# The order of every engine's instructions written out as a table

## The chip, the cores and the metric

The kernel runs on one core of a Trainium2 chip. The core has five engines that work side by side and meet at semaphores: TensorE (PE) for matrix products, VectorE (DVE) and ScalarE (ACT) for elementwise work, GpSimd (POOL), and SyncE (SP), which here only issues DMA transfers. Every engine takes its instructions in one fixed order; one that has to wait holds up all that stand behind it on the same engine. The metric is the device time of the whole program in microseconds; of several executions the median counts.

## What is computed

One inference step of a one-layer decoder for a prompt of 1024 tokens and a sample group of 8 x 8 tokens (1088 columns in all), all in float32:

```python
h = rmsnorm(x, norm_mix)
q, k, v, gu, gv, ga, gb = split_in(h @ w_in)
o = sink_attention(...)             # window of 128, 16 heads on 4 key heads, learned sinks
vn = layernorm(gelu(gv), ln_g, ln_b)
s = spatial_gating(gelu(gu), vn, ws, bs)       # 128 x 128 lower triangles, 6 groups
merged = sigmoid(ga) * (o @ w_pa) + sigmoid(gb) * (s @ w_pb)
x = x + merged @ w_out
f = conv_ffn(rmsnorm(x, norm_ffn), ...)        # up, causal conv of width 3, gelu gate, down
y = rmsnorm(x + f, norm_final)
```

Besides y the new keys, values, convolution rows and normalised v rows are returned.

## The kernel before

Activations lie with features on the 128 partitions and tokens along the free dimension. A float32 product is made of three products of rounded halves: `split` writes hi, a copy by ACT (L41), and lo = src - hi, by DVE (also L41), for weights (`wh`, `wl`), activations (`th`, `tl`, `t` for both in one tile) and softmax results (`ph`, `pl`). PE then adds wh*hi, wh*lo and wl*hi.

The large products save multiplications: seven products of half-sized blocks instead of eight (class `Chain`). A chain works on 288 tokens (group 0, tiles `t`) or 256 (group 1, `th`, `tl`); with both groups two chains take turns. Product j writes the PSUM bank given by the j-th letter of "adadaca", so j=2, 4 and 6 go on in the bank of j=0. Before PE may go on there, ACT has copied the sum so far out of it (`keep`, L296 and L298: `k1`, `k5`, `ku`, and `kn` with the sign changed). DVE adds finished parts into `z` (L303, L339), ACT copies others (L343).

The stages in order: v and gv token by token (L535); the input chains for ga, gb, q, k, gu (L317), with the layer norm's jobs (L758 to L765: load `v` from DRAM, ACT L759, DVE L761 and L762, store) and the mixing matmuls (L788, L816) woven in between; attention of group 0, then group 1, with pieces of the merge products (L242) between its steps; the output product; the up projection chains (L317) with convolution and gate (L1564 to L1631); the down projection (L1686); the final norm (L1719 to L1772).

One attention step: scores (PE L1182), copy and mask (ACT L1188, DVE L1190), row maximum (DVE L1196), four exponentials (ACT L1199), reciprocal and scaling of `s` (DVE L1201, L1202), transposes (PE L1209) into `pt`, split into `ph` and `pl`, product with the values (PE L1233) into `po`, of which there is one bank; ACT copies one half of it to `ot` (L1238), two DVE additions make `of` (L1243), and a split makes `oh` and `ol`. Merge products leave their bank (`mm`, two of them) by a DVE multiplication into `stg` (L1030 in the branch, L1054 in the merge), which is then stored.

The order of each engine comes from the tile framework's scheduler: it takes the instructions as written and lets those that are ready pass others. A handful are pinned with `keep_in_program_order` (splits of the mixing's results, some additions of the down projection, a table load, the last outputs). DMA transfers are issued by SP in the order so found. Weights are loaded through a ring of raw tiles and split up to three products ahead (`W.get(3, ...)`).

Of the kernel before, what the change touches and what calls it, by code (L numbers as in the profile page):

```python
# [6 lines left out]
F32 = mybir.dt.float32  # L7
F32R = mybir.dt.float32r
I32 = mybir.dt.int32
AF = mybir.ActivationFunctionType  # L10
# [5 lines left out]
P = 128  # L16
# [18 lines left out]
def layer(tc, a):  # L35
    nc = tc.nc
    V, S, G, PE = nc.vector, nc.scalar, nc.gpsimd, nc.tensor

    def split(hi, lo, src, pin=False):

        for x in (S.copy(hi, src), V.tensor_sub(lo, src, hi.bitcast(F32))):  # L41
            if pin:
                tc.keep_in_program_order(x)

# [4 lines left out]
    with ExitStack() as top:  # L49
# [14 lines left out]
        warm = cst.tile([P, 1], F32, name="c_warm")  # L64
# [318 lines left out]
        with ExitStack() as ph1:  # L383
            c1 = ph1.enter_context(tc.tile_pool(name="c1", bufs=1))
# [57 lines left out]
            order = [*range(FEW, 9), 0, *range(9, 15), 1, *range(15, NFF), 2]  # L442
# [14 lines left out]
            def dn_unit(j, i):  # L457
# [12 lines left out]
                def add(to, x, y):  # L470
                    tc.keep_in_program_order(V.tensor_add(to, x, y))
                    return to
# [388 lines left out]
            s_raw = {}  # L861
# [5 lines left out]

            def split_s(g, pool, c, pin=False):
                x = pool.tile([P, 2, groups[g]["n"]], F32R, name=f"s{g}{c}")
                split(x[:, 0], x[:, 1], s_raw.pop(c), pin)  # L870
                ss[g].append((x[:, 0], x[:, 1]))
# [87 lines left out]
            for at, (pair, gs) in enumerate(seq):  # L959
# [12 lines left out]
                for j in range(7):  # L972
                    w = W.get(3, 1 if j < 4 else 4 if at == len(seq) - 1 else 2)
# [87 lines left out]
            def attention(gr, pieces):  # L1061
# [18 lines left out]
                if has_s:  # L1080
                    st = {}

                    def sc_s(kc):
# [19 lines left out]
                        if kc == 0:  # L1103
                            tc.keep_in_program_order(S.activation(warm, s2[:, 3, 0:1], AF.Exp))
                        for lo, hi, m in ((0, P, smp["m"][:, None, 0:P].to_broadcast([P, 4, P])),
# [165 lines left out]
            for c in range(3):  # L1271
                split_s(1, m1, c, True)
                load_s(1, c + 2)
# [363 lines left out]
        for at, f in enumerate(order):  # L1637
# [11 lines left out]
            for j in range(7):  # L1649
                w = W.get(3, 1)  # L1650
# [10 lines left out]
        with ExitStack() as ph3:  # L1661
# [85 lines left out]
            def y_out(th, e, c0, c1):  # L1747
                lo, hi = spans[e]
                w, at = hi - lo, KD * (HT * th + lo)
                tc.keep_in_program_order(  # L1750
                    nc.sync.dma_start(a["y"][:, at + c0 * w:at + c1 * w].rearrange("p (m t) -> p m t", t=w),
                                      x1[c0 // 4, th, e][:, c0 % 4:c0 % 4 + c1 - c0]))

            def fin_copy(th, e, rb):
                rs = lp.tile([P, 288], F32, name="rb", bufs=2)[:, :spans[e][1] - spans[e][0]]
                copy = S.copy(rs, rb[-1])
                if not (th and e):
                    tc.keep_in_program_order(copy)
                return rb[0], rs

            def fin_mul(th, e, by, cs, eng=V):
                w = spans[e][1] - spans[e][0]
                for c in cs:
                    x2 = x1[c // 4, th, e][:, c % 4:c % 4 + 2]
                    x = eng.tensor_mul(x2, x2, by[:, None, :].to_broadcast([P, 2, w]))
                    if eng is V:
                        tc.keep_in_program_order(x)

# [93 lines left out]
        tops.close()  # L1862
        tops.close()


# [89 lines left out]
```

## Time and profile before

| | us |
|---|---|
| median of 3 executions | 1509.08 |
| the three | 1508.57, 1509.08, 1514.09 |
| the profiled execution, its own time | 1507.61 |
| its span in the profile | 1505.9 |
| PE busy | 1491.5 |
| PE loading weights | 1451.8 |
| DVE busy | 1176.4 |
| ACT busy | 856.3 |
| POOL busy | 265.7 |

A timeline row gives the start, the time it took, engine, source line, operation, tile written and tiles read, shape, how many instructions the row merges, and in brackets the idle time before it with what ended that. A window's row gives the stretch, its length, then for PE, weight loads, DVE, ACT and POOL the busy time and the number of instructions, and last the granted clock, the share of time that DMA engines were busy, and GB/s. Names lose their buffer numbers. Ends of matmuls are modelled, so PE counts as busy a little beyond the time in which it takes in columns.

### The profile page before, as it was taken

To read this page: it belongs to the slowest core of one execution; us is meant where nothing else is said; L and a number is where in the kernel's file an instruction comes from. 1 tells how busy PE (TensorE), PEld (TensorE's weight loads), DVE (VectorE), ACT (ScalarE), POOL (GpSimd) and SP (SyncE) were. 2 spreads that over 40 slices of the span, in tenths; PEclk is the share of its full clock that TensorE was granted. 3 is DMA by queue.
4 is the path that set the end of the run, shared out by engine and by line. 5 is a ranking of instruction groups with operands and counts; after the bars stand their busy time and mean duration, and the time that the engine had idled before them with its cause. 6 is when DMAs were issued, how large, how long until landed. Compare 5 with 4: busy or idle time off the path is not lost.

```text
span 1505.9 us, 30082 instructions
## 1 busy us (share of the span) xinstructions
PE 1491.5 (99%) x11508; PEld 1451.8 (96%) x11508; DVE 1176.4 (78%) x1886; ACT 856.3 (57%) x1790; POOL 265.7 (18%) x375
## 2 busy tenths in 40 slices
PE   9999999999999999999999999999999999999998
PEld 9999999999998989998989999999999999999998
DVE  7798776755576887989667988898899888785586
ACT  7657676654465765864443555555555556363464
POOL 0001000110030222320134321332242222000002
PEclk9999999999999999999999999999999999999999
DMA  7688446864779757438988423232242226993453
GB/s 253 225 275 274 155 163 224 243 207 150 239 243 294 219 180 231 162 123 308 335 295 287 141 109 122 98 142 108 83 151 109 84 83 223 326 303 98 113 172 148
DMA packets 134431, 289.88 MB, mean 192 GB/s; under 512 B 15760, under 2 KB 36560, under 8 KB 134288
## 3 DMA queue, kind: packets, MB, share of 16 engines
q1 hardware_dynamic: 134144, 287.96, 56.8%
q8 instruction: 90, 1.47, 0.4%
q14 instruction: 53, 0.43, 0.1%
q10 hardware_dynamic: 144, 0.01, 0.0%
HBM read 198.97 MB, written 90.92 MB: 192 GB/s over the span
## 4 chain that ended last, share of the span: by engine, by line
PE 85%; DVE 5%; ACT 4%; DMA 3%; issue 2%; POOL 1%; SPq 0%; POOLq 0%; ACTq 0%; DVEq 0%
PE st L317 45%; PE dn L1686 14%; PE mm L242 13%; PE st L535 6%; PE po L1233 2%; PE sc L1182 1%; DVE wl L41 1%; PE pt L1209 1%; DMA v<-gvd 1%; PE mx L816 1%; ACT wh L41 1%; ACT s L1199 1%; DMA kd<-q 0%; DMA v<-gvds 0%; DVE v L761 0%
## 5 line engine op out<-in xcount | busy, mean ns | idle before, releaser
L317 PE MATMUL st<-t,wh 128*128 128x288 f32 x2128 | 428.6, 295 | 3.4 <-ACT k L296 2.3
L317 PEld LDWEIGHTS st<-t,wh 128*128 128x128 f32 x2128 | 335.7, 188 | 4.6 <-ACT k L296 3.0
L317 PE MATMUL st<-t,wl 128*128 128x288 f32 x1064 | 312.2, 293 | 0.0
L317 PE MATMUL st<-th,wh 128*128 128x256 f32 x1064 | 296.0, 278 | 0.6 <-ACT k L296 0.5
L317 PE MATMUL st<-tl,wh 128*128 128x256 f32 x1064 | 294.7, 277 | 0.0
L317 PE MATMUL st<-th,wl 128*128 128x256 f32 x1064 | 294.5, 277 | 0.0
L317 PEld LDWEIGHTS st<-th,wh 128*128 128x128 f32 x1064 | 200.0, 188 | 1.9 <-ACT k L296 1.4
L317 PEld LDWEIGHTS st<-t,wl 128*128 128x128 f32 x1064 | 200.1, 188 | 0.0
L317 PEld LDWEIGHTS st<-th,wl 128*128 128x128 f32 x1064 | 199.8, 188 | 0.0
L317 PEld LDWEIGHTS st<-tl,wh 128*128 128x128 f32 x1064 | 199.8, 188 | 0.0
L1686 PE MATMUL dn<-th,wh 128*128 128x288 f32 (+1 forms) x616 | 177.1, 288 | 0.6 <-ACT zb L343 0.6
L1686 PE MATMUL dn<-tl,wh 128*128 128x288 f32 (+1 forms) x616 | 176.8, 287 | 0.0
L41 ACT CAST wh<-wraw 128x512 fp32r<-128x512 f32 (+2 forms) x188 | 129.4, 701 | 82.0 <-DMA wraw<-wt 30.1
L1686 PE MATMUL dn<-th,wl 128*128 128x288 f32 (+1 forms) x616 | 175.3, 285 | 0.0
L41 DVE TENSOR_TENSOR wl<-wraw,wh 128x512 fp32r<-128x512 f32 (+2 forms) x188 | 148.0, 800 | 28.5 <-ACT wh L41 26.2
L41 ACT CAST wh<-ws 128x512 fp32r<-128x512 f32 x168 | 102.5, 621 | 93.9 <-PE st L317 53.0
L41 DVE TENSOR_TENSOR wl<-ws,wh 128x512 fp32r<-128x512 f32 x168 | 117.5, 710 | 44.5 <-ACT wh L41 43.7
L1686 PEld LDWEIGHTS dn<-th,wh 128*128 128x128 f32 x616 | 115.7, 188 | 1.0 <-ACT zb L343 0.8
L1686 PEld LDWEIGHTS dn<-th,wl 128*128 128x128 f32 x616 | 116.1, 188 | 0.1
L1686 PEld LDWEIGHTS dn<-tl,wh 128*128 128x128 f32 x616 | 115.7, 188 | 0.1
L535 PE MATMUL st<-w2h,hh 128*128 128x256 f32 x288 | 80.6, 280 | 0.4 <-ACT rst L501 0.4
L535 PE MATMUL st<-w2h,hl 128*128 128x256 f32 x288 | 80.1, 279 | 0.1
(281 smaller groups left out, 3169.1 us busy)
## 6 DMA issues: line engine op xcount, KB each, us to landing
wraw<-wt SPq DMA_DIRECT2D x137, 512.0 KB
traw<-td SPq DMA_DIRECT2D x77, 272.0 KB
td<-za SPq DMA_DIRECT2D x22, 544.0 KB
q<-qd SPq DMA_DIRECT2D x16, 512.0 KB
upd<-hl SPq DMA_DIRECT2D x14, 512.0 KB
td<-t SPq DMA_DIRECT2D x11, 544.0 KB
wpart<-wt SPq DMA_DIRECT2D x22, 256.0 KB
qd<-q SPq DMA_DIRECT2D x8, 576.0 KB
```

The source lines that it names most:

```text
L41: for x in (S.copy(hi, src), V.tensor_sub(lo, src, hi.bitcast(F32))):
L242: PE.matmul(ps[:, lo:lo + c1 - c0], u[:, k, :], v[:, c0:c1], start=(k == 0 and i == 0), stop=(k == nk - 1 and i == 2))
L317: PE.matmul(ps, u[:, kk, :], v, start=first and kk + i == 0, stop=kk == 3 and i == 2, skip_group_check=True)
L535: PE.matmul(ps, u[:, lo:lo + P], v[:, k, :], start=k + i == 0, stop=k == KD - 1 and i == 2)
L816: PE.matmul(ps[:, P * i:P * i + P], vn[:, i], late["wst"][:, c, :], start=True, stop=True)
L1182: PE.matmul(ps[:, h, o0:256], q, kst[kv][:, e, k0:cur + P], start=e == 0, stop=e == 1)
L1199: S.activation(s[:, h], s[:, h], AF.Exp, bias=nm[:, h:h + 1], accum_out=dn[:, h:h + 1])
L1209: PE.transpose(pt[:, h * P:h * P + P], s[:, h, 0:P], ident)
L1233: PE.matmul(po, v[:, kv, :], t, start=e == 0, stop=last)
L1686: PE.matmul(place(m, e), u[:, m, :], v[:, lo:hi], start=new and i + k == 0 and (e == 0 or m % 2 == 0), stop=i == NU - 1 and k == 2, skip_g ...
```

## The change

All calls of `keep_in_program_order` go. After the program is written, a new function binds each engine's instructions into one chain: each depends, without a semaphore, on the one before it in the table's order. A digit of the table says how many places ahead of the next unplaced instruction, in the order as written, the next one is taken from.

```diff
-            if pin:
-                tc.keep_in_program_order(x)
...
-                    tc.keep_in_program_order(S.copy(th, x))
+                    S.copy(th, x)
...
+        issue_order(tc)
+
+def issue_order(tc):
+    import re
+    engines = {}
+    for i in tc.nc.cur_bb.bb.instructions:
+        if not isinstance(i, mybir.BassTilePoolBoundary):
+            engines.setdefault(str(i.engine).split(".")[-1], []).append(i)
+    for name, text in ORDER.items():
+        left, last = engines[name], None
+        steps = []
+        for run, far, one in re.findall(r"\((\d+)\)|\[(\d+)\]|([.0-9a-zA-Z])", text):
+            steps += [0] * int(run) if run else [int(far) if far else max(0, DIGITS.find(one))]
+        for j in steps + [0] * (len(left) - len(steps)):
+            now = left.pop(j)
+            if last is not None:
+                tc.add_manual_dep(
+                    now, last.name,
+                    mybir.DependencyInfo(mybir.DependencyClass.NoSync, mybir.DependencyReason.DATA),
+                    reason="issue order")
+            last = now
+
+ORDER = {
...
+    "Activation": (
+        "1.2(4)b..91.7.1.4..22.1...1(5)223..3(4)1..1.1..1.37..1.3..1..133..1(5)777cc.b..e1e.2.a3.33.22.4."
...
+}
```

What is computed and by which instructions does not change. PE's order is the same row for row. Against the order before, 2 instructions stand elsewhere on POOL, 68 on ACT, 132 on DVE and 28 on SP, counted as the fewest that have to be moved to turn one order into the other. Nearly all pass only a few neighbours. In the listings below line numbers of the changed kernel are one or two lower than before, for lines that the change removes.

ACT in the stage of the input chains, before. `k1_4137` copies a chain's bank `st_4124` after its product j=0; `v_4158` and `v_4242` are the layer norm's activations, `z` and `wh` finished outputs and weight casts:

```order
L343 ACTIVATE z10_3806<-st_3815 128x288
L759 ACTIVATE v_4158<-v_4158,mr_3857,sd_3856 128x768
L852 ACTIVATE z10_3806<-z10_3806 128x576
L343 ACTIVATE z11_3808<-st_3830 128x256
L41 CAST wh_4248<-wraw_3706 128x512
L852 ACTIVATE z11_3808<-z11_3808 128x512
L296 COPY k1_4137<-st_4124 128x288
L759 ACTIVATE v_4242<-v_4242,mr_3857,sd_3856 128x768
```

And now:

```order
L341 ACTIVATE z10_3806<-st_3815 128x288
L850 ACTIVATE z01_3807<-z01_3807 128x512
L294 COPY k1_4137<-st_4124 128x288
L757 ACTIVATE v_4158<-v_4158,mr_3857,sd_3856 128x768
L850 ACTIVATE z10_3806<-z10_3806 128x576
L341 ACTIVATE z11_3808<-st_3830 128x256
L294 COPY k1_4152<-st_4139 128x256
L40 CAST wh_4248<-wraw_3706 128x512
L850 ACTIVATE z11_3808<-z11_3808 128x512
```

The copy has passed the activation of v, two of z, a copy and a weight cast; the other chain's copy `k1_4152` has come forward too. Two more waits of this stage (for `kn_4296` and `k1_4413`) are treated alike: the copies now stand ahead of the activations of `v_4314` and `v_4434`.

DVE in attention, before. `stg_7237` empties a merge product's bank `mm_7302`, `dn` and `s_7324` finish a softmax, `of_7369` reads the bank `po_7351`:

```order
L41 TENSOR_TENSOR pl_7359<-pt_7353,ph_7358 128x512
L1030 TENSOR_TENSOR stg_7237<-stg_7237,mm_7302 128x576
L1201 RECIPROCAL dn_7330<-dn_7330 128x4
L1243 TENSOR_TENSOR of_7369<-po_7351,ot_7367 64x256
L1202 TENSOR_TENSOR s_7324<-s_7324,dn_7330 128x4x128
L1243 TENSOR_TENSOR of_7369<-po_7351,ot_7367 64x256
L1190 COPY_PREDICATED s_7397<-c_mprev_482,sc_7388 128x4x128
L41 TENSOR_TENSOR ol2_6587<-of_7369,oh2_6586 128x2x128
L1196 TENSOR_REDUCE nm_7401<-s_7397 128x4
```

And now:

```order
L41 TENSOR_TENSOR pl_7359<-pt_7353,ph_7358 128x512
L1199 RECIPROCAL dn_7330<-dn_7330 128x4
L1200 TENSOR_TENSOR s_7324<-s_7324,dn_7330 128x4x128
L1241 TENSOR_TENSOR of_7369<-po_7351,ot_7367 64x256 x2
L1188 COPY_PREDICATED s_7397<-c_mprev_482,sc_7388 128x4x128
L41 TENSOR_TENSOR ol2_6587<-of_7369,oh2_6586 128x2x128
L1194 TENSOR_REDUCE nm_7401<-s_7397 128x4
L1028 TENSOR_TENSOR stg_7237<-stg_7237,mm_7302 128x576
```

The bank's evacuation went from the front to the end of the step, and `s` ahead of both halves of `of`. Other steps of attention change likewise; the six evacuations `stg` that move back pass 4 to 17 places, and weight splits up to 5.

ACT between the last up projection chain and the down projection, before. `zb_16256` copies the chain's last sum out of `st_16265`, `c_16596` is a convolution's first step:

```order
L41 CAST th_16490<-traw_16405 128x544
L41 CAST wh_16496<-wraw_16419 128x512
L1564 ACTIVATE c_16596<-za_16255,cw_11020 128x1104
L343 ACTIVATE zb_16256<-st_16265 128x256
L41 CAST wh_16496<-wraw_16494 128x512
```

And now:

```order
L40 CAST th_16490<-traw_16405 128x544
L40 CAST wh_16496<-wraw_16419 128x512
L341 ACTIVATE zb_16256<-st_16265 128x256
L1562 ACTIVATE c_16596<-za_16255,cw_11020 128x1104
L40 CAST wh_16496<-wraw_16494 128x512
```

The copy and the convolution have changed places. On SP, at the program's start, the load of the second feature block `x1` has passed the load of the second part of `x0`; later a number of loads pass stores that wait for results, by one to six places.

More of the change, by code (lines that the diff above doesn't have):

```diff
@@ L37, in layer, with split @@
     V, S, G, PE = nc.vector, nc.scalar, nc.gpsimd, nc.tensor
-    def split(hi, lo, src, pin=False):
-        for x in (S.copy(hi, src), V.tensor_sub(lo, src, hi.bitcast(F32))):
-            if pin:
-                tc.keep_in_program_order(x)
+    def split(hi, lo, src):
+        S.copy(hi, src)
+        V.tensor_sub(lo, src, hi.bitcast(F32))
     def scale_split(hi, lo, src, by):
@@ L1103, in sc_s @@
                         if kc == 0:
[L1104 removed]
+                            S.activation(warm, s2[:, 3, 0:1], AF.Exp)
                         for lo, hi, m in ((0, P, smp["m"][:, None, 0:P].to_broadcast([P, 4, P])),
@@ L1749, in y_out @@
                 w, at = hi - lo, KD * (HT * th + lo)
[L1750 to L1752 removed]
+                nc.sync.dma_start(a["y"][:, at + c0 * w:at + c1 * w].rearrange("p (m t) -> p m t", t=w),
+                                  x1[c0 // 4, th, e][:, c0 % 4:c0 % 4 + c1 - c0])
             def fin_copy(th, e, rb):
                 rs = lp.tile([P, 288], F32, name="rb", bufs=2)[:, :spans[e][1] - spans[e][0]]
[L1756 to L1758 removed]
+                S.copy(rs, rb[-1])
                 return rb[0], rs
```

73 lines of the change are left out of this document (66 added, 7 removed).

## The prediction

> **What bounds the kernel now.** I read the page first, then the list of waits of TensorE (PE), then the timeline around each wait. The page's span, its row of busy times, and the last row of PE's timeline:
>
> ```profile
> span 1505.9 us, 30082 instructions
> ...
> PE 1491.5 (99%) x11508; PEld 1451.8 (96%) x11508; DVE 1176.4 (78%) x1886; ACT 856.3 (57%) x1790; POOL 265.7 (18%) x375
> ...
> 1499.66 0.61 PE L1731 MATMUL fs<-c_ident,rt 128*128 128x128 f32 x4
> ```
>
> PE is busy for 1491.5 of 1505.9 us, so all that any order of the other engines can win is in the 14.4 us of idle PE and in what "busy" conceals. The last matmul is over at 1500.3; the 5.6 us behind it are the output's. The waits of PE, whole span (who waited, for whom, us, times, longest):
>
> ```profile
> PE st L317 <- ACT k L296: 2.8, 4, 1.5
> PE st L590 <- DVE c_ones L69: 1.2, 1, 1.2
> PE st L317 <- ACT kn L298: 1.0, 1, 1.0
> PE pt L1209 <- DVE s L1202: 0.6, 2, 0.4
> PE dn L1686 <- ACT zb L343: 0.6, 1, 0.6
> PE fs L1731 <- DVE rt L1723: 0.6, 1, 0.6
> PE pt L1123 <- DVE s L1116: 0.4, 1, 0.4
> PE st L535 <- ACT rst L501: 0.4, 1, 0.4
> PE mm L242 <- DVE x1g L1360: 0.2, 1, 0.2
> PE po L1233 <- DVE of L1243: 0.2, 1, 0.2
> ```
>
> Of these 8.0 us, the memset at the start (c_ones), rst and rt stay as they are: 2.2 us. The other seven rows, 5.8 us in 11 waits, are all for PSUM evacuations or softmax results of ScalarE (ACT) and VectorE (DVE), and the new table puts just these ahead of neighbours. So the question is how much of 5.8 us comes free, and what each wait costs beyond its listed idle time.
>
> Four rows of PE's timeline show the second thing:
>
> ```profile
> 293.74 0.28 PE L317 MATMUL st<-tl,wh 128*128 128x256 f32 x1
> 293.86 0.28 PE L317 MATMUL st<-th,wl 128*128 128x256 f32 x1
> 294.99 0.53 PE L317 MATMUL st<-t,wh 128*128 128x288 f32 x2 [0.86 <-ACT k L296]
> 295.37 0.29 PE L317 MATMUL st<-t,wl 128*128 128x288 f32 x1
> ```
>
> Matmuls of 256 columns start 0.12 us apart, so the next was due at 293.98 and came 1.01 late, not 0.86: a listed wait hides about 0.15. After it two matmuls take 0.38 where two of 288 columns take about 0.26 when PE runs through: another 0.12. I count each listed wait as its idle time plus 0.27.
>
> **Stage 280 to 330 us: minus 4.2.** Here the first pass of seven-product chains runs (one product per j, two chains), while the layer norm's jobs use the same ACT. Two windows, all engines:
>
> ```profile
> 230.00:280.00 50.00, 50.00 (x411) 50.00 (x411) 33.37 (x61) 29.87 (x61) 4.28 (x4) 1.00 0.68 229
> 280.00:330.00 50.00, 46.64 (x374) 45.90 (x374) 35.15 (x49) 28.06 (x55) 7.59 (x7) 1.00 0.73 223
> ```
>
> 411 matmuls in 50 us is 0.122 each; 374 need 45.5, so 4.5 us are lost. From the listed waits: two for k (2.3) and one for kn (1.0), 3.3 + 3 x 0.27 = 4.1. ACT rows from the approach to the three waits:
>
> ```profile
> 290.92 0.63 ACT L852 ACTIVATE z<-z 128x512 f32<-128x512 f32 x1 [0.85 <-DVE z L303]
> ...
> 294.55 0.39 ACT L296 COPY k<-st 128x288 f32<-128x288 f32 x1
> ...
> 303.69 1.03 ACT L759 ACTIVATE v<-v,mr,sd 128x768 f32<-128x768 f32 x1 [4.83 <-DMA v<-gvd]
> ...
> 307.74 0.67 ACT L298 ACTIVATE kn<-st 128x288 f32<-128x288 f32 x2
> ...
> 315.85 1.03 ACT L759 ACTIVATE v<-v,mr,sd 128x768 f32<-128x768 f32 x1 [1.18 <-DMA v<-gvd]
> ```
>
> The k copy of j=0 frees the bank in which j=2 goes on. Between the end of its product and the stall PE ran the other chain's j=0 and both chains' j=1, 36 matmuls x 0.122 = 4.4 us, so the copy could have run from 289.6 on and waited for nothing but its place. In the new order it stands right behind the row of 290.92, about 291.5, and PE asks for it at 293.98: the wait goes whole. kn frees a bank in the same way. It now stands ahead of the activation that waits for a transfer until 303.69; its first half ends at 308.1 (two copies in 0.67 from 307.74), the stall began 1.3 before, its product 4.4 before that, at about 302.4, so it runs some 5 us earlier. The third wait, the longest, is for a k behind the activation of 315.85; k goes ahead of it, more than 2.5 us earlier for a stall of 1.5 + 0.15, and that activation falls nine places back. What is late next is the layer norm's v, read by the mixing matmuls of a later stage. Between 4.1 and 4.5 I take 4.2.
>
> **Attention, 460 to 670 us: minus 3.1.** The edit repeats one pattern. DVE and PE rows of one step:
>
> ```profile
> 542.54 0.76 DVE L1030 TENSOR_TENSOR stg<-stg,mm 128x576 f32<-128x576 f32 x1 [0.45 <-PE mm L242]
> ...
> 543.65 0.42 DVE L1243 TENSOR_TENSOR of<-po,ot 64x256 f32<-64x256 f32 x1 [0.27 <-ACT ot L1238]
> 543.99 0.68 DVE L1202 TENSOR_TENSOR s<-s,dn 128x512 f32<-128x512 f32 x1
> 544.70 0.42 DVE L1243 TENSOR_TENSOR of<-po,ot 64x256 f32<-64x256 f32 x1
> ...
> 544.81 0.30 PE L1209 MATMUL pt<-c_ident,s 128*128 128x128 f32 x1
> 545.26 0.47 PE L1233 MATMUL po<-ph,vst 128*128 128x512 f32 x1
> ```
>
> The transposes at 544.81 wait for s, the matmul at 545.26 for the second of, which frees the one po bank. Now reciprocal and s go first (s over by about 543.4), both of follow (over by about 544.4 instead of 545.1), and stg, whose result is only stored, comes last: this step gains some 0.5. Listed for such steps are s 0.6 and 0.4 and of 0.2, four waits: 1.2 + 4 x 0.27 = 2.3. The wait at 544.81 is under 0.15 and not listed; there are many like it. The page leaves at most 14.4 - 8.0 - 5.6 = 0.8 us of unlisted idle time, and each hides its 0.15 as well, so I bound them by 0 and 2 here and take 1.0, near the middle, as the step above has one of each. One of the two s waits loses only one short DVE instruction ahead of it, so I leave 0.2 of it. 2.3 + 1.0 - 0.2 = 3.1.
>
> **Single places elsewhere: minus 3.1.** The two other k waits, 2.8 - 2.3 = 0.5 + 2 x 0.27 = 1.0; x1g 0.2 + 0.27 = 0.5; unlisted ones before further k copies and in the tail, 0 to 2, taken as 1.0 like those above. The zb wait is different:
>
> ```profile
> 1264.80 1.32 ACT L1564 ACTIVATE c<-za,cw 128x1104 f32<-128x1104 f32 x1
> 1266.01 0.37 ACT L343 ACTIVATE zb<-st 128x256 f32<-128x256 f32 x1
> ...
> 1265.16 0.28 PE L317 MATMUL st<-th,wl 128*128 128x256 f32 x1
> ...
> 1266.43 0.39 PE L1686 MATMUL dn<-th,wh 128*128 128x256 f32 x1 [0.60 <-ACT zb L343]
> ```
>
> zb moves ahead of the 1.32 us convolution, but its product ends only at 1265.44, so it runs until about 1265.8 and PE resumes 0.6 earlier, not 1.2. The convolution then starts 1.0 late, hidden because the transfers that follow it feed the down projection's later units. 1.0 + 0.5 + 1.0 + 0.6 = 3.1.
>
> **What costs.** At the head SP now loads x1 ahead of x0's second part. ACT keeps its order:
>
> ```profile
> 5.68 0.51 ACT L46 ACTIVATE hh<-x,c_gains 128x256 fp32r<-128x256 f32 x1 [0.93 <-DMA x<-xt]
> 6.39 0.78 ACT L46 ACTIVATE hh<-x,c_gains 128x576 fp32r<-128x576 f32 x1 [0.20 <-DMA x<-xt]
> ...
> 6.73 0.28 PE L535 MATMUL st<-w2h,hh 128*128 128x256 f32 x1
> ```
>
> If the parts change landing places, x0's part lands at 6.39 instead of 5.68 and its hh ends at 6.90, after PE wants it at 6.73; the lo half follows. Bounds: 0 and +0.7; I take +0.3, as PE stalls for x1 a little later anyway. Elsewhere what moves back are weight casts (one to five places), stores, and evacuations that are only stored. The longest move is stg at 648.03, seventeen places, past the work that fills this window:
>
> ```profile
> 648.03 0.76 DVE L1054 TENSOR_TENSOR stg<-stg,mm 128x576 f32<-128x576 f32 x1 [0.33 <-PE mm L242]
> ...
> 647.70:657.70 10.00, 10.00 (x72) 9.24 (x71) 9.49 (x18) 8.18 (x27) 2.73 (x6) 1.00 0.34 111
> ...
> 660.60 0.43 PE L242 MATMUL mm<-oh,wh 128*128 128x320 f32 x2
> ```
>
> So it ends near 657.7, and the product that reuses its bank starts at 660.60: 2.9 us of cover. Weights are cast three products ahead in the chains. I count these at nothing singly, but with PE 10 us nearer to everything some new short waits will appear; the nearest price is a shortest listed wait, 0.2 + 0.27, and I take three of them, +1.4, with 0 and +6 as bounds.
>
> **Sum:** -4.2 - 3.1 - 3.1 + 0.3 + 1.4 = -8.7. The profiled execution took 1507.61, so 1498.9; from the median of the three runs, 1509.08, it is 1500.4. The two are executions of one kernel; I forecast their middle, 1499.6.
>
> [...]
>
> **Rivals.**
> - *Given back, 1504.6.* The layer norm's activations wait for transfers (303.69, 315.85), which no order speeds up; PE could meet them 4.2 us earlier and wait there. DVE in attention is full (9.49 of 10.00), so half of 3.1 could fail too. -8.7 + 4.2 + 1.5 = -3.0 from either time. For it: those two rows. Against: the chains' matmuls read none of those v tiles.
> - *More hidden waits, 1495.* If the short waits are at their upper bounds (1.0 and 1.0 more), the first stage gives its 4.5, and nothing is given back (1.4) or lost at the head (0.3), the sum is -8.7 - 2.0 - 0.3 - 1.4 - 0.3 = -12.7: 1494.9 from the profiled time. [...]
> - *Slower, 1513.* Six PSUM evacuations in attention fall four to seventeen places back behind a full DVE. Should DVE slip more than the 2.9 us of cover, the next product but one waits for its bank behind work that is now ahead of it, 2 x 0.42 + 0.68 + 0.27 = 1.8 us each time: 6 x 1.8 = 10.8, and attention's 3.1 does not come: -8.7 + 3.1 + 10.8 = +5.2, 1512.8 from the profiled time, 1514.3 from the median. It decides once a moved-back stg ends after the next product but one begins. Against: DVE's total work is unchanged.
> - *Not doing what it says* (the pins are gone, but order holds by dependencies alone): PE's order is unchanged row for row, and the moved rows do stand as described, so I give this nothing.
>
> **How the numbers follow.** Forecast (1496 to 1503) 0.62, given back 0.20, more 0.10, slower 0.08. A run of this kernel tells 0.5% (7.5 us: below 1501.5, above 1516.6) from no change. Faster: 0.85 of the forecast plus all of "more", 0.63; slower: half of that rival, 0.04; same the rest, 0.33. The range reaches from 1495.0 (upper bounds of the terms) to 1508.0 (given back, plus 3 of the +6).
>
> **What would show it.** In the new profile the listed waits of PE for k and kn between 280 and 330 should be gone and that window hold about 405 matmuls; s, of and x1g should drop out of the list; zb should shrink to under 0.1; PE's busy time should stay near 1490 and the span near 1498. Wrong would be: PE waits for v, wh or wl that are not there now, a wait for stg before L242, or the same waits at other times.

## The result and the profile after

| | before | changed |
|---|---|---|
| median, us (runs) | 1507.76 (8) | 1502.40 (8) |
| lowest to highest | 1506.85 to 1514.09 | 1501.15 to 1504.10 |
| profiled execution, its own time | 1507.61 | 1502.30 |

The ratio of the times is 0.996, with a 95% interval of 0.9947 to 0.9973: the change makes the kernel about 0.4% faster, 5.4 us. The forecast was 1499.6, a gain of 8.7 on some 1508.3, so 3.3 us of the gain did not come. The median lies above the 1501.5 under which the prediction called the kernel faster (0.63), and so in the part that it called the same (0.33), although the interval excludes 1. In the changed kernel's source each line of the kernel stands up to seven lines higher (L317 is L315, L1233 is L1231, L1741 is L1739); the instructions are the same.

From the page of the changed kernel, the span and the row of busy times:

```profile
span 1500.6 us, 30059 instructions
...
PE 1487.9 (99%) x11508; PEld 1451.1 (97%) x11508; DVE 1180.2 (79%) x1886; ACT 856.2 (57%) x1790; POOL 272.4 (18%) x375
```

The span is 5.3 us shorter. PE's idle time, span less busy, went from 14.4 to 12.7 only; the other 3.6 us are less busy time, in part because matmuls right behind a wait took longer too, as the prediction's rows of 293 to 295 us show: two took 0.38 for 0.26 (its window of 280 to 330 had 46.64 us of busy PE for 45.5 us of work). POOL's busy time grew from 265.7 to 272.4, though no work was added to it. Now the list of PE's waits (waiter, whom for, us in total, times, longest):

```profile
PE fs L1739 <- DVE acc L1706: 1.5, 1, 1.5
PE st L588 <- DVE c_ones L67: 1.2, 1, 1.2
PE po L1231 <- POOL cl L1217: 1.0, 3, 0.4
PE st L533 <- ACT hh L44: 0.7, 1, 0.7
PE st L315 <- ACT k L294: 0.6, 2, 0.4
PE fs L1729 <- DVE rt L1721: 0.6, 1, 0.6
PE po L1231 <- ACT s L1197: 0.4, 1, 0.4
PE sc L1087 <- DVE z L337: 0.4, 1, 0.4
PE st L533 <- ACT rst L499: 0.4, 1, 0.4
PE po L1123 <- DVE of L1144: 0.3, 1, 0.3
```

Of the seven rows that were to go, kn, zb, both s of DVE, x1g and the `of` of L1243 have left it, and k has fallen from 2.8 to 0.6. Six rows are new: acc, cl, hh, the s of ACT, z and another `of`. The window of the stage in which most was to be won (stretch, length, then PE, weight loads, DVE, ACT, POOL with their instructions, granted clock, share of the DMA engines, GB/s):

```profile
280.00:330.00 50.00, 50.00 (x411) 50.00 (x410) 33.31 (x50) 29.54 (x57) 6.82 (x7) 1.00 0.68 214
```

411 matmuls where there were 374: PE now runs this stage at the pace that it had from 230 to 280 us before (411 in 50 us).

PE's order is the same in all kernels of this study, so each matmul can be compared with itself (each row of the table below is one profiled execution). The matmul that sums `acc` for the last rows started at 1490.76 before and 1484.72 now, a lead of 6.04. The table gives the change of this lead, stage by stage, worked out from the first matmul of each stage in the two traces (times are those of the kernel before; minus is gained on it; the row "kernel" is the changed one, the others are the experiments below):

| | 130-180 | 275-330 | 330-460 | 460-600 | 600-668 | 668-1290 | 1290-1475 | 1475-1492 |
|---|---|---|---|---|---|---|---|---|
| kernel | -0.54 | -4.57 | +1.91 | -2.49 | +0.60 | -2.43 | -0.12 | +1.37 |
| e1 | +2.03 | -4.57 | +0.45 | +0.28 | +0.27 | +0.15 | -0.12 | -0.01 |
| e2 | -0.40 | -1.73 | +0.68 | -2.42 | +0.57 | -0.18 | -0.12 | 0.00 |
| e3 | -0.54 | -4.57 | +2.64 | -2.47 | +0.15 | -2.44 | +0.84 | +0.01 |
| e4 | -0.54 | -4.58 | -0.05 | -2.54 | +0.12 | -2.38 | -0.12 | +1.37 |
| e5 | +1.48 | -2.06 | -0.31 | +0.39 | +5.84 | -0.08 | -0.12 | 0.00 |
| e6 | -0.32 | -4.57 | +2.53 | -2.48 | +0.60 | -1.15 | +2.82 | +1.36 |
| e7 | -0.11 | -4.57 | -0.31 | -2.08 | +0.15 | -2.13 | +0.51 | +0.01 |
| e8 | -0.54 | -4.57 | +1.13 | -2.60 | +0.61 | -2.62 | +1.44 | +1.37 |
| e9 | -0.54 | -4.58 | +3.30 | -2.50 | +0.61 | -1.89 | +3.20 | +1.49 |
| e10 | -0.54 | -4.57 | +1.81 | -2.48 | +0.09 | -2.25 | +3.69 | +0.11 |
| e11 | -0.54 | -4.58 | +0.48 | -2.16 | +0.56 | -2.68 | +0.43 | 0.00 |

With +0.24 before 130 us the row of the changed kernel sums to -6.0; the last eight matmuls of its profile then ran at a granted clock of 0.59 and cost 0.8, which leaves the 5.3 of the span. So the gain came where it was expected, and 3.9 us were given back: 1.9 at 330 to 460, 0.6 at 600 to 668 and 1.4 at the very end. The experiments ask why.

### The profile page after: what moved, and what is told of

Its sections match the earlier page's. It is cut to its first block, busy times and chain, and to the rows that moved or that the text cites. A ratio compares the mean times of both kernels' runs of the same rounds, so it can differ in the third digit from the quotient of the medians.

```text
span 1500.6 us, 30059 instructions
## 1 busy us (share of the span) xinstructions
PE 1487.9 (99%) x11508; PEld 1451.1 (97%) x11508; DVE 1180.2 (79%) x1886; ACT 856.2 (57%) x1790; POOL 272.4 (18%) x375
## 4 chain that ended last, share of the span: by engine, by line
PE 93%; DMA 2%; DVE 2%; ACT 1%; issue 1%; POOL 1%; SPq 0%; POOLq 0%; ACTq 0%; DVEq 0%
PE st L315 50%; PE mm L240 16%; PE dn L1684 14%; PE st L533 7%; PE po L1231 2%; PE sc L1180 2%; PE pt L1207 1%; DMA wl<-upd 1%; PE mx L814 1%; DMA sg1d<-z 0%; DMA x1d<-x1g 0%; DMA x<-xt 0%; POOL cl L1217 0%; DVE pl L41 0%; ACT wh L40 0%
## 5 line engine op out<-in xcount | busy, mean ns | idle before, releaser
L315 PE MATMUL st<-t,wh 128*128 128x288 f32 x2128 | 427.6, 294 | 0.0
L315 PEld LDWEIGHTS st<-t,wh 128*128 128x128 f32 x2128 | 335.5, 188 | 0.1
L315 PE MATMUL st<-t,wl 128*128 128x288 f32 x1064 | 311.9, 293 | 0.0
L315 PE MATMUL st<-th,wh 128*128 128x256 f32 x1064 | 295.2, 278 | 0.6 <-ACT k L294 0.6
L315 PE MATMUL st<-tl,wh 128*128 128x256 f32 x1064 | 294.4, 277 | 0.0
L315 PE MATMUL st<-th,wl 128*128 128x256 f32 x1064 | 294.1, 276 | 0.0
L315 PEld LDWEIGHTS st<-th,wh 128*128 128x128 f32 x1064 | 199.8, 188 | 1.4 <-ACT k L294 1.2
L315 PEld LDWEIGHTS st<-t,wl 128*128 128x128 f32 x1064 | 199.7, 188 | 0.3 <-DMA wl<-upd 0.3
L315 PEld LDWEIGHTS st<-th,wl 128*128 128x128 f32 x1064 | 199.9, 188 | 0.0
L315 PEld LDWEIGHTS st<-tl,wh 128*128 128x128 f32 x1064 | 199.8, 188 | 0.0
```

The source lines that it names most:

```text
L315: PE.matmul(ps, u[:, kk, :], v, start=first and kk + i == 0, stop=kk == 3 and i == 2, skip_group_check=True)
```

## The experiments

Each is the changed kernel or the kernel before with another table. "Before" and "changed" are orders of engines; nothing is left out of the computation. Times are medians with the number of runs; the ratio is to the kernel before, run beside it.

| | kernel | us (runs) | ratio, 95% interval |
|---|---|---|---|
| e1 | before, 283-340 us changed | 1505.38 (10) | 0.9976, 0.9960 to 0.9992 |
| e2 | before, 455-672 us changed | 1505.31 (10) | 0.9983, 0.9967 to 1.0000 |
| e3 | changed, end as before | 1502.91 (8) | 0.9955, 0.9938 to 0.9971 |
| e4 | changed, 425-452 us as before | 1500.57 (7) | 0.9944, 0.9925 to 0.9964 |
| e5 | before, five splits moved up | 1512.48 (1) | none; before beside it 1507.91 |
| e6 | changed, three `of` put back | 1504.36 (10) | 0.9979, 0.9968 to 0.9989 |
| e7 | changed, all three pieces back | 1498.86 (6) | 0.9941, 0.9926 to 0.9956 |
| e8 | changed, two places on ACT back | 1502.64 (6) | 0.9955, 0.9938 to 0.9972 |
| e9 | changed, loads on SP back | 1503.85 (8) | 0.9959, 0.9942 to 0.9975 |
| e10 | changed, `of` and end back | 1500.95 (8) | 0.9948, 0.9930 to 0.9966 |
| e11 | changed, 425-452 us and end back | 1499.48 (6) | 0.9954, 0.9942 to 0.9965 |

The intervals are as wide as the effects, so what follows is read from the table of leads; where a time does not bear it out, that is said.

### e1: the chains' copies alone

```diff
+L294 COPY k1_4137<-st_4124 128x288
 L757 ACTIVATE v_4158<-v_4158,mr_3857,sd_3856 128x768
...
-L294 COPY k1_4137<-st_4124 128x288
```

> The order before, but for the moves of ScalarE, VectorE and the DMA queue between 283 and 340 us. Theory (each term stands by itself): the three waits for k and kn go, TensorE is 4.2 to 4.6 us ahead from 330 us on, and nothing takes that back, since the waits given back at 425 to 455, in attention and at the end come from moves made there: the time is 4.2 to 4.6 us under the kernel before. Rival (given back): transfers and casts of 425 to 455 us keep their own pace, so TensorE meets them 4.5 us earlier and waits there some 1.7 us: the time is 2.5 to 3 us under the kernel before, with waits of TensorE for k at 425 to 445.

Its stage gained 4.57, as in the changed kernel to the hundredth, and only 0.45 went again up to 460 us. The rival's mechanism is out: what is won from k and kn is not waited for later, and its waits for k at 425 to 445 are not in the list. Its time, 2.5 us under the kernel before, is nevertheless the rival's: as the last section shows, the old order loses less in this stage in other executions than in the profile of before, so the stage is worth less than 4.57 on average. That its profile is only 1.25 ahead at the end has another cause, 2.03 us lost at 130 to 180, where its order is that of before. There two k copies came late in that execution, by 1.0 and 1.1 us. In the kernel's own profile of before they did not.

### e2: attention alone

```diff
-L1028 TENSOR_TENSOR stg_7237<-stg_7237,mm_7302 128x576
 L1199 RECIPROCAL dn_7330<-dn_7330 128x4
+L1200 TENSOR_TENSOR s_7324<-s_7324,dn_7330 128x4x128
 L1241 TENSOR_TENSOR of_7369<-po_7351,ot_7367 64x256
-L1200 TENSOR_TENSOR s_7324<-s_7324,dn_7330 128x4x128
...
+L1028 TENSOR_TENSOR stg_7237<-stg_7237,mm_7302 128x576
```

> The order before, but for the moves between 455 and 672 us. Theory: attention's own moves make both its gain and its loss. The four listed waits for s and of go and TensorE gains some 2.3 us up to 600, then loses some 0.6 to 1.5 in waits for POOL's cl behind weight splits, as in the changed kernel, three cl of about 1.56 us: 1.5 to 2 us under the kernel before. Rival: the waits for cl arise because TensorE arrives some 5 us earlier from other stages; then they are absent here, all cl take about 0.64, and the time is 3.1 us under the kernel before.

The other steps from 455 to 672 us are as changed too. From 460 to 668 it gained 1.85, against 1.89 in the changed kernel, and its list of waits has cl with 1.0 us in three waits although PE arrives there 1.7 us later than in the changed kernel. The waits for cl come from attention's own moves, not from PE's being early. The time, 2.6 us under the kernel before, lies between the theory's 2 and the rival's 3.1 and does not decide.

### e5 and e6: what slows POOL's cl

In attention POOL masks `cl`, made from DVE's `pl`, for PE's last product of a step. Three of the 28 cl took 1.56 us. One of them in the changed kernel, DVE, then POOL, then PE:

```profile
607.40 0.69 DVE L41 TENSOR_TENSOR pl<-pt,ph 128x512 fp32r<-128x512 f32 x1 [0.17 <-ACT ph L40]
608.01 1.22 DVE L41 TENSOR_TENSOR wl<-wraw,wh 128x1024 fp32r<-128x1024 f32 x1
```

```profile
608.16 1.56 POOL L1217 TENSOR_SCALAR_AFFINE_SELECT cl<-pl 128x512 fp32r<-128x512 f32 x1 [0.16 <-DVE pl L41]
```

```profile
609.77 0.50 PE L1231 MATMUL po<-cl,dvst 128*128 128x512 f32 x1 [0.37 <-POOL cl L1217]
```

And POOL and DVE in the kernel before, at a place where the second half of `of` follows pl and cl took 0.63:

```profile
608.03 0.63 POOL L1219 TENSOR_SCALAR_AFFINE_SELECT cl<-pl 128x512 fp32r<-128x512 f32 x1 [0.25 <-DVE pl L41]
```

```profile
607.22 0.68 DVE L41 TENSOR_TENSOR pl<-pt,ph 128x512 fp32r<-128x512 f32 x1
607.82 0.84 DVE L1243 TENSOR_TENSOR of<-po,ot 64x256 f32<-64x256 f32 x2
```

Since `of` was moved ahead of pl, a weight split wl of 128x1024 now starts right before cl in three steps, and cl ends 0.49 after it. That is the suspicion; e5 makes it alone, in the kernel before:

```diff
 L41 TENSOR_TENSOR pl_8279<-pt_8273,ph_8278 128x512
+L41 TENSOR_TENSOR wl_8708<-wraw_8296,wh_8707 128x1024
 L1241 TENSOR_TENSOR of_8289<-po_8269,ot_8287 64x256
-L41 TENSOR_TENSOR wl_8708<-wraw_8296,wh_8707 128x1024
...
```

> The order before, with one thing changed on VectorE: in five steps of attention (612, 627, 636, 651 and 661 us) the weight split wl of 128x1024 is put directly behind pl, ahead of the second half of of, so that it runs while GpSimd masks cl; the places of pl and of everything on GpSimd stay. Theory (lock-out): GpSimd's masking of cl, which takes 0.64 in these steps of the kernel before, starts at the same time as wl and ends only some 0.5 us after wl is over, so the five cl take about 1.5 each. Rival (late pl): cl was late in the changed kernel only because pl came behind of; then the five cl keep 0.64, as pl is where it was.

Three cl took 1.56, two kept 0.64. One of each kind, DVE, POOL and PE:

```profile
612.43 1.21 DVE L41 TENSOR_TENSOR wl<-wraw,wh 128x1024 fp32r<-128x1024 f32 x1
...
638.23 1.59 DVE L41 TENSOR_TENSOR wl<-wraw,wh 128x1024 fp32r<-128x1024 f32 x1 [0.19 <-ACT wh L40]
```

```profile
612.57 1.56 POOL L1217 TENSOR_SCALAR_AFFINE_SELECT cl<-pl 128x512 fp32r<-128x512 f32 x1 [0.40 <-DVE pl L41]
...
638.11 0.64 POOL L1217 TENSOR_SCALAR_AFFINE_SELECT cl<-pl 128x512 fp32r<-128x512 f32 x1 [0.16 <-DVE pl L41]
```

```profile
614.23 0.48 PE L1231 MATMUL po<-ph,vst 128*128 128x512 f32 x1 [1.06 <-DVE of L1241]
```

The two exceptions say more than the three hits. At 638 (and at 665 alike) the split waited for its wh and started 0.12 after cl: cl kept its 0.64 and the split took 1.59, 0.38 longer. At 612, and in the three steps of the changed kernel, the split started first, by 0.14 or 0.15, took 1.21 or 1.22, and cl took 1.56. So in each of these six steps the one that started first kept its length, and the other was held. What the two contend for, no run shows. PE, though, waited five times 1.0 to 1.5 us, by its pace, for `of`, which the split had pushed back: 5.84 us lost from 600 to 668. So `of`'s place in the step is worth more than cl's.

e6 goes the other way: in the changed kernel the three `of` stand between pl and wl again.

```diff
-L1241 TENSOR_TENSOR of<-po,ot 64x256
 L41 TENSOR_TENSOR pl<-pt,ph 128x512
+L1241 TENSOR_TENSOR of<-po,ot 64x256
 L41 TENSOR_TENSOR wl<-wraw,wh 128x1024
...
```

> The changed kernel, with one thing put back on VectorE: in the three steps whose cl took 1.56 us, the second half of of stands between pl and the weight split wl again, as before. Theory (lock-out): the three cl take 0.64 to 0.75, TensorE's three waits for cl (1.0 us listed, 1.5 by its pace) go, and no wait for of takes their place: 1.0 to 1.5 us under the changed kernel. Rival: TensorE reaches these products earlier than before and meets cl or of anyway; then waits for cl or of of about 0.3 each remain at the same places and the time is within 0.5 us of the changed kernel.

All cl are short again (the group of cl on POOL: ns shortest, median, longest):

```profile
L1217 POOL TENSOR_SCALAR_AFFINE_SELECT cl<-pl x28: 637/637/758, 497.1 to 662.9; 128x512 fp32r<-128x512 f32 x28
```

And the waits for cl are gone from the list. But nothing was won: +0.60 from 600 to 668, as in the changed kernel. PE gained 0.5 to 0.7 at each of the three places and lost it again in the following steps in pieces of 0.1 to 0.2. The theory had the length of cl right and its price wrong; the rival had the price right, with other waits than it named. Over all profiles, attention from 460 to 668 gained 1.99 on average in the seven with the waits for cl (1.60 to 2.42) and 2.07 in the three without (1.88 to 2.39). The spread within both groups is mostly one wait of 0.5 us that has nothing to do with cl; it is explained below, under attention. The time of e6 is not used: its profile has a slow stretch in the down projection, which its order does not explain (below).

### e3: the end

DVE and POOL of the changed kernel before the last rows of sums, and PE:

```profile
1482.26 0.67 DVE L1760 TENSOR_TENSOR x<-x,fs 128x512 f32<-128x512 f32 x1
1482.85 0.44 DVE L1694 TENSOR_TENSOR x<-x,dn 128x288 f32<-128x288 f32 x1
1483.22 1.45 DVE L1706 TENSOR_TENSOR acc<-acc,sq 128x288 f32<-128x288 f32 x1
```

```profile
1478.61 5.74 POOL L1760 TENSOR_TENSOR x<-x,rb 128x576 f32<-128x576 f32 x4 [219.17 <-ACT rb L1753]
```

```profile
1484.72 0.75 PE L1739 MATMUL fs<-acc,c_ones 128*128 128x288 f32 x2 [1.49 <-DVE acc L1706]
```

PE wanted acc at about 1483.1, where its products run out. The addition started at 1483.22 because a scaling of finished outputs (1482.26) now stands between two additions of bank results, and it took 1.45, until 0.3 after POOL's four multiplications end at 1484.35. In e3 the scalings go in pairs behind the additions again; three splits ahead of them, a reciprocal and a copy by ACT also go back:

```diff
 L1706 TENSOR_TENSOR acc_16746<-acc_16746,sq 128x288
-L1694 TENSOR_TENSOR x_17062<-x_17062,dn 128x288
-L1760 TENSOR_TENSOR x_16747<-x_16747,fs 128x512
-L1694 TENSOR_TENSOR x_17062<-x_17062,dn 128x288
+L1760 TENSOR_TENSOR x_16747<-x_16747,fs 128x512 x2
+L1694 TENSOR_TENSOR x_17062<-x_17062,dn 128x288 x2
 L1706 TENSOR_TENSOR acc_16746<-acc_16746,sq 128x288
-L1760 TENSOR_TENSOR x_16747<-x_16747,fs 128x512
...
```

> The changed kernel, with the order of VectorE and ScalarE from 1476 us of the kernel before on (the last seventy instructions) as before. Theory (order): the wait of TensorE for acc before the last rows of sums goes from 1.5 back to some 0.3 us, and the time is 1.2 to 1.6 us under the changed kernel. Rival (collision): the addition acc took 1.44 us instead of 0.46 because GpSimd's multiplications by rb ran beside it; they do so in any order, so acc takes 0.8 or more again, the wait shrinks by at most half, and the time is 0.3 to 0.8 us under the changed kernel.

DVE of e3:

```profile
1480.69 0.45 DVE L1706 TENSOR_TENSOR acc<-acc,sq 128x288 f32<-128x288 f32 x1
...
1482.26 0.81 DVE L1694 TENSOR_TENSOR x<-x,dn 128x288 f32<-128x288 f32 x2
1483.22 0.80 DVE L1706 TENSOR_TENSOR acc<-acc,sq 128x288 f32<-128x288 f32 x1
```

The end lost nothing against before (+0.01, and +1.37 in the changed kernel), and acc left the list of waits. Two causes share the 1.37: the later start, 0.72 by PE's pace (acc starts at 1483.22 in both, but PE arrives 0.72 later in e3), and the collision with POOL, which costs 0.65 more in the changed order: an addition before POOL's work took 0.46 (e3 at 1478.37, POOL from 1479.32), this one 0.80 in e3, as before, and 1.45 in the changed kernel. The acc ahead of it takes 1.02 there and 0.45 in e3 (its row at 1480.69, with POOL at work too), so part of the later start may be collision too. That it is POOL that holds it is read from these rows; no run took POOL's work away. Every profile with the changed end lost 1.36 to 1.49 there, the four with the end put back 0.00 to 0.11. Its time does not show it: the median, 1502.91, is not under that of the changed kernel. In the profiled execution, 1500.92, there were 0.96 us lost at 1290 to 1300, where a DVE step waited 3.48 us for a transfer (2.41 in the changed kernel); whether the other executions lost it there too is not known.

### e4, e8, e9: 425 to 452 us

ACT of the changed kernel, and PE:

```profile
428.00 0.61 ACT L40 CAST wh<-ws 128x512 fp32r<-128x512 f32 x1
428.52 0.64 ACT L294 COPY k<-st 128x256 f32<-128x256 f32 x2
...
437.75 0.67 ACT L40 CAST s<-stg 128x576 fp32r<-128x576 f32 x1 [1.19 <-DMA stg<-sd]
```

```profile
428.25 0.28 PE L315 MATMUL st<-th,wl 128*128 128x256 f32 x1
428.94 0.38 PE L315 MATMUL st<-th,wh 128*128 128x256 f32 x1 [0.42 <-ACT k L294]
```

Here the table did the opposite of what it did at 290 us: the cast of 428.00 has passed the copy that PE waits for. The next copies stand behind a cast that waits for a transfer (437.75) and behind a sigmoid. e4 puts this stretch back on three engines; ACT's part:

```diff
-L40 CAST s00_5962<-stg_5898 128x576
 L852 ACTIVATE z00_5517<-z00_5517 128x576
...
+L40 CAST s00_5962<-stg_5898 128x576
...
+L294 COPY k1_5825<-st_5812 128x256
 L40 CAST wh_5943<-ws_5945 128x512
-L294 COPY k1_5825<-st_5812 128x256
...
+L852 ACTIVATE z01_5807<-z01_5807 128x512
...
-L852 ACTIVATE z01_5807<-z01_5807 128x512
 L294 COPY k5_6027<-st_6014 128x256
```

> The changed kernel, with the order of ScalarE, VectorE and the DMA queue between 425 and 452 us as before. Theory (order): the copies k1 and k5 of the last chains lost their places to a weight cast and a sigmoid there; put back, the three waits of TensorE for k (1.1 us in all with their restarts) go, and most of the 1.7 us that TensorE loses at 425 to 455: 1.1 to 1.7 us under the changed kernel. Rival (late transfers): ScalarE is held by casts that wait for the sd transfers, which come at their own time; TensorE waits for k all the same, and the time is within 0.5 us of the changed kernel.

330 to 460 us now loses nothing (-0.05): 1.96 us better, a bit more than the theory had. Four profiles with this stretch as changed lost 1.81 to 2.64 (mean 2.2), three with it as before -0.31 to +0.48 (mean 0.0); e1, e2 and e5, which never had the changed stretch, -0.31 to +0.68. e8 puts back the copy `k1_5825` and the sigmoid `z01_5807` alone, as in the last rows of that diff; e9 the loads alone, on SP:

```diff
-L896 DMA cache<-ckt 128x1024
-L864 DMA stg<-sd_173 128x576
 L854 DMA sg1d_141<-z_5518 128x576
...
+L864 DMA stg<-sd_173 128x576
+L143 DMA wraw<-wt 128x1024
+L896 DMA cache<-ckt 128x1024
 L864 DMA stg<-sd_174 128x576
```

> The changed kernel with two places of ScalarE alone put back between 428 and 443 us: the copy k1 stands ahead of a weight cast again, and the sigmoid of z01 ahead of the second k1, not between it and the copy k5. Nothing moves on VectorE or the DMA queue. Theory (copies): TensorE's waits for k at 428.94 (0.58) and 440.58 (0.35), by its pace, go, and TensorE is 0.9 us or more ahead at 446 us against the changed kernel; the wait of 455 us for a sum by VectorE stays, at 0.5 to 1.0. Rival (loads): the later splits and loads set the pace there; then the waits for k move to the next copies and TensorE is less than 0.4 us ahead at 446 us, the rest of the 2.0 us being the order of the loads.

> The changed kernel with the DMA queue alone put back between 429 and 433 us of the kernel before: the load of cache stands behind five other transfers again, not ahead of them, and the load of the second s part behind two stores. ScalarE and VectorE keep the changed order. Theory (loads): the transfers sd that ScalarE's casts wait for come earlier; ScalarE's wait of 1.19 us for one of them shrinks to 0.3 or less, the k copies behind it are in time, and TensorE is 0.8 us or more ahead of the changed kernel at 458 us, though the wait of 428.9 for k1 (0.58) stays. Rival (copies): only the two places on ScalarE matter; TensorE is within 0.3 us of the changed kernel at 458 us.

e8: the wait of 428.9 is gone, but PE was only 0.4 ahead of the changed kernel at 446 us, at the rival's bound and not the theory's 0.9, and 0.8 over the whole stage (1.13 for 1.91): ACT still waited 0.98 us for the sd transfer, and the next copy was late by 0.44. e9 missed outright. The loads alone made it worse, 3.30 for 1.91, as ACT's first s cast, which the table has moved up, now waited longer for its transfer (0.38 in the changed kernel):

```profile
433.75 0.68 ACT L40 CAST s<-stg 128x576 fp32r<-128x576 f32 x1 [2.43 <-DMA stg<-sd]
```

A second wait, for a sum z of DVE (L337) at 455 us, is in the lists of the changed kernel, e3, e6, e8 and e9 with 0.4 to 1.0 us, and in those of e4, e7 and e11 it is not. So neither engine's order explains the 2.2 us by itself. The casts of s were moved up on ACT together with their loads on SP; put back together, with three places on DVE, they cost nothing. Which of the moved loads matters was not tried.

### e10, e7, e11: the pieces together

Their edits are those of e3, e4 and e6: e10 has e3's and e6's, e7 all three, e11 e3's and e4's.

> The changed kernel with of put back between pl and wl in the three steps of attention and the last seventy instructions as before, but 425 to 452 us as changed. Theory (each loss stands by itself): TensorE gains some 0.9 to 1.3 us at 603 to 650 us and 1.4 us before the last rows of sums, so 2.3 to 2.7 under the changed kernel in all, about 1500, and the kernel with all three pieces put back stays some 2 us below this one. Rival: what the two give depends on the piece that is left as changed, and together they give less than the 1.4 us of the end alone.

> The changed kernel with all three pieces put back: the order before at 425 to 452 us, of between pl and wl in the three steps of attention, and the last seventy instructions of VectorE and ScalarE. Theory (the losses are separate and each is made by its own moves): 2.0 + 1.3 + 1.4 = 4.7 us under the changed kernel, about 1498 and some 0.65% under the kernel before, with TensorE's list of waits without k at 425 to 445, cl and acc. Rival (what is put right early is waited for later): the time is no better than the best single piece, 1.8 us under the changed kernel, and new waits of the size of those removed stand further on.

> The changed kernel with 425 to 452 us and the last seventy instructions as before, but attention as changed, with wl directly behind pl and its three waits for cl. Theory (of put back is worth nothing): between 460 and 668 us TensorE gains 1.9 to 2.4 us on the kernel before, as in the profiles with of put back, because of comes later there and is waited for in small pieces; the time is within 0.5 us of the kernel with three pieces put back, about 1499, and no worse than the better of the two single pieces. Rival (the waits for cl count in full): TensorE gains 1 to 1.4 us less than with of put back between 603 and 650 us, and the time is about 1500.

e10 kept the end's 1.4 (+0.11), gained nothing at 600 to 668 that e3 and e4 have not without `of` put back (+0.09, beside +0.15 and +0.12), so the theory's 0.9 to 1.3 there did not come, and the loss at 330 to 460 stayed (+1.81): the end and that stretch do stand by themselves. e7 has all three. It is 3.5 us under the changed kernel for the 4.7 expected, since `of`'s 1.3 are not to be had; its list of waits is nearly empty:

```profile
PE st L588 <- DVE c_ones L67: 1.2, 1, 1.2
PE fs L1729 <- DVE rt L1721: 0.6, 1, 0.6
PE st L533 <- ACT hh L44: 0.4, 1, 0.4
PE st L533 <- ACT rst L499: 0.4, 1, 0.4
PE po L1123 <- DVE of L1144: 0.2, 1, 0.2
...
```

e11 leaves `of` as changed, keeps its three waits for cl, and is within 0.6 us of e7 (1499.48 and 1498.86): from 460 to 668 it gained 1.60, e7 1.93. That is a little short of the 1.9 to 2.4 expected, by the one wait of 0.5 us named before, and the 1 to 1.4 us of the rival did not come. Both beat the kernel before and the changed one, at some 3 us under the latter's median; between the two the runs don't decide.

## Why the prediction was right and where not

**Stage 280 to 330, -4.2:** right in cause, and in size against the profile that it was worked out from. Measured -4.57 in all ten profiles with this order, with 411 matmuls in the window for the 405 named. Against e2 and e5, two more executions of the old order in this stage, it is only -2.84 and -2.51, so for the median the term was too large. The rival "given back" put its loss on the layer norm's activations; e1 shows no such loss, so its 1504.6, nearer to the result than the forecast (2.2 against 2.8 us), was near by luck in this part. Its other part, that half of attention's 3.1 could fail, came near what was measured.

**Single places, -3.1:** right. 130 to 180, 668 to 1290 and 1290 to 1475 sum to -3.1 (0.54 + 2.43 + 0.12). Only zb was to shrink to under 0.1 and still costs 0.25 by PE's pace.

**Attention, -3.1:** the gain was -2.5, up to 600 us, and from 600 to 668 it turned into +0.6; net -1.9. The step costed each moved reciprocal and s, and took for granted that DVE's other instructions fill in behind at no price. The waits for cl, new as they are, are not the reason, as e6 shows. Most of the 0.6 is a single wait. DVE, POOL and PE of the changed kernel, and then of e3, whose attention is in the same order:

```profile
601.56 0.87 DVE L41 TENSOR_TENSOR ol<-of,oh 128x256 fp32r<-128x256 f32 x1
601.52 0.64 POOL L1217 TENSOR_SCALAR_AFFINE_SELECT ch<-ph 128x512 fp32r<-128x512 f32 x1 [0.42 <-ACT ph L40]
603.89 0.48 PE L1231 MATMUL po<-ph,vst 128*128 128x512 f32 x1 [0.36 <-ACT s L1197]
```

```profile
601.77 0.41 DVE L41 TENSOR_TENSOR ol<-of,oh 128x256 fp32r<-128x256 f32 x1
601.73 0.94 POOL L1217 TENSOR_SCALAR_AFFINE_SELECT ch<-ph 128x512 fp32r<-128x512 f32 x1 [0.43 <-ACT ph L40]
603.64 0.47 PE L1231 MATMUL po<-ph,vst 128*128 128x512 f32 x1
```

DVE's split `ol` has come to stand beside POOL's mask `ch`; in the order of before pl stands there. One of the two is held. Where it is `ol`, 0.87 for 0.41, all that follows on DVE comes later, and PE waits. (The list puts this wait down to ACT's s, but the second `of`, which frees the bank, ends at 603.80 and s at 603.61.) Of the ten profiles with attention as changed or with `of` alone put back, six have the long `ol` and this wait, and lost 0.56 to 0.61 from 600 to 668 us; four have the long `ch`, 0.90 to 0.96, and no such wait, and lost 0.09 to 0.15. The two start within 0.04 us of each other, so one order has both outcomes. At equal outcome the waits for cl make no difference: 0.56 to 0.61 with them and 0.60 without, 0.12 and 0.15 with them and 0.09 and 0.15 without.

So 0.5 us of what attention lacks is this collision. Some 0.7 us are missing without it too (e3 and e4 gained 2.32 and 2.42 from 460 to 668). That what one step gains the next one waits for is the reading I take of that rest; no run took work off DVE.

**Head, +0.3:** the delay came as described: the second hh starts at 6.43 and the matmul that was to run at 6.73 starts at 6.99, with a listed wait of 0.7. Its price is not told apart from nothing. The lead before 130 us changed by +0.24 here, by -0.29 to +1.34 in the eight other profiles with this SP order, and by -0.30 to +0.27 in e1, e2 and e5, whose SP order is that of before.

**What costs, +1.4:** the step that failed. The term was three new waits of 0.47 from the price of a shortest listed wait, "I count these at nothing singly". Measured were 1.9 at 425 to 452 and 1.4 at the end, 3.3 us without attention's 0.6. The bounds of 0 and +6 held it; the value taken did not come from a place. Two of the places, at 428 and 440, could have been read from the order beforehand: a weight cast that passes a k copy is the mirror image of the edit that was costed at 290 us. Put back alone they gave 0.8 of the 1.9 (e8). The third, acc, needed POOL's row beside DVE's.

**Slower:** its mechanism did not show. No wait for stg stands ahead of L240, though the six evacuations moved as described; 2.9 us of cover were enough.

The sum would then have been -4.57 - 1.9 - 3.1 + 0.24 + 3.3 = -6.0, and with 0.8 for the last matmuls the span's -5.3. Of the signs named for a wrong step, "the same waits at other times" is the one that came: k at 428 to 441.

## What to carry to other kernels

When a table moves many instructions, look for moves against the rule that the gains rest on, at each place where the bottleneck engine takes over a bank, and price those singly; a flat sum for "some new waits" is the weakest term of the forecast. Where two engines hold each other, as POOL and DVE do here, look at what now stands beside what, not only at what stands behind what. And do not credit a removed wait before the steps behind it have been looked at: in attention three waits, 1.0 us in all, could be removed or put back with no change of the time.

## What the runs showed of the hardware that was not expected

**POOL and DVE hold each other.** cl took 0.64 or 1.56 us, wl 1.21 or 1.59, ch 0.64 or 0.94, ol 0.41 or 0.87, by which of the two engines was at work when the other came; the addition acc with 0.45, 0.80 or 1.45 looks alike. Where the two start within 0.04 us of each other, as ch and ol do, the outcome changes from execution to execution and with it 0.5 us of the time. The time appears as a longer instruction, not as a wait of either engine, so the list of waits names only the one that is waited for.

**One order, several executions.** With the order of before, the stage of 280 to 330 lost 1.7 and 2.1 us less in e2 and e5 than in the profile of before (-1.73 and -2.06 in the table, with nothing changed there), and 130 to 180 varied from -0.40 to +2.03. Windows of e2 and e5:

```profile
280.00:330.00 50.00, 48.22 (x388) 47.46 (x388) 36.69 (x52) 28.97 (x57) 6.97 (x7) 1.00 0.70 219
```

```profile
280.00:330.00 50.00, 48.28 (x391) 47.81 (x390) 35.91 (x51) 28.86 (x56) 6.96 (x7) 1.00 0.73 224
```

So the waits for k that the forecast removed are not 3.3 us in every execution. With the changed order the same stage came out alike to 0.01 us ten times. That an instruction waiting for a transfer no longer stands ahead of the copies would explain both; it was not tried by itself.

**Two paces of PE.** The last eight matmuls took 1.92 to 2.08 us in four of the thirteen profiles and 1.16 in the others. The window around them in the changed kernel, and in the kernel before:

```profile
1492.90:1495.00 2.10, 1.92 (x8) 1.63 (x8) 0.94 (x3) 0.00 (x0) 0.00 (x0) 0.59 0.76 312
```

```profile
1498.90:1500.30 1.40, 1.16 (x8) 0.97 (x8) 0.60 (x2) 0.00 (x0) 0.00 (x0) 1.00 1.01 411
```

The granted clock was 0.59 in the one and 1.00 in the other; e2 had the slow pace too (2.08 us, at a granted clock of 0.50), and its end is ordered as before. Ahead of these matmuls PE has only short ones and a wait of 0.55, from 1489.6 to 1493.1 us in the changed kernel; in the kernel before it has the same, from 1495.6 to 1499.1 us, and the clock was 1.00. What lowers the clock no run shows. The other slow stretch is not of this kind. In e6, e9 and e10 the down projection ran 1.7% slower from about 1290 to 1480 us, at a granted clock of 1.00. The window of e9 and that of the changed kernel:

```profile
1350.00:1400.00 50.00, 50.00 (x402) 50.00 (x401) 27.79 (x50) 20.20 (x35) 0.00 (x0) 1.00 0.35 92
```

```profile
1350.00:1400.00 50.00, 50.00 (x409) 50.00 (x409) 27.53 (x49) 19.16 (x33) 0.00 (x0) 1.00 0.35 98
```

402 matmuls for 409, which is about the 2.9 to 3.8 us that these three lost from 1290 to 1475 us against the changed kernel. What causes it stays open.
